# A decoder layer on one core: two weight splits moved into the merge and kept in DRAM, an engine order written out at the end of the mix

## The chip, the core and the metric

The kernel runs on one core of a Trainium2 chip. The core has five engines with a queue of instructions each: PE (TensorE, matrix products), DVE (VectorE, element by element), ACT (ScalarE, functions and scalings), POOL (GpSimd, element by element) and SP (SyncE, which here only starts DMA transfers). ACT and POOL can start DMA transfers too. Each engine runs its own queue in order and waits for the others through semaphores. SBUF is the on-chip memory of 128 partitions; PSUM holds the products in banks of 128 x 512 float32. DRAM is reached by DMA only. The metric is the device time of one execution in microseconds (us); less is better.

## The reference

One layer of a decoder on x of 1024 positions by 1024 channels, all in float32:

```python
xn = rmsnorm(x, norm_mix_w[l])
proj = xn @ w_in[l]
da_q, da_k, da_v, sw_q, sw_k, sw_v, g_da, g_sw = split_cols(proj)
...
y_da = diff_attention(da_q, da_k, da_v, lam, lam_init, subln_w[l])
y_sw = sliding_window_attention(sw_q, sw_k, sw_v, sinks[l])
merged = jax.nn.sigmoid(g_da) * (y_da @ w_br_da[l]) + jax.nn.sigmoid(g_sw) * (y_sw @ w_br_sw[l])
x = x + merged @ w_mix_out[l]
xn = rmsnorm(x, norm_ffn_w[l])
x = x + conv_ffn(xn, w_up[l], conv_w[l], conv_b[l], w_down[l])
return rmsnorm(x, norm_final_w)
```

`conv_ffn` is `u = xn @ w_up` (1024 to 5632), a causal convolution of width 3 along the positions, `silu(gate) * val`, and `@ w_down`. The change lies in the lines of `merged`, of `merged @ w_mix_out` and at the start of `xn @ w_up`.

## The kernel before, in words

**Products.** Channels lie on the partitions, positions along the free axis, in two halves (`hf` 0 and 1) of 512. A float32 product is made of three products of a faster type: each operand is split into a high part (a cast, on ACT) and a low part (what the cast left out, a subtraction, on DVE), and hi x hi, hi x lo and lo x hi are added in PSUM. `split`, `load_w` (L177 and L179) and `part_pair` (L125 and L127) make such parts; they are called splits below. On top of it stands one level of Strassen-Winograd: a product of 2 x 2 blocks takes seven block products P1 to P7 instead of eight, of operands that are blocks (A11, A12, A22; B11, B21, B22) or sums of blocks (S1 to S4; T1 to T4).

**Stages.** By time in the trace: projection (0 to 235), attention (to 507), merge (to 594.7), mix (to 672.5), the pairs of the up product (to 1107), the down product (to 1331). 

**Merge** (`rest`). Eight steps m, one per 128 channels. SP loads two stored gates `gr` (L845), POOL multiplies them by the rstd (L846), ACT takes the sigmoid, PE makes the two branch products (`sc`, `g`), DVE multiplies the gates into them as it takes them out of PSUM (L860, L862), POOL (DVE for the last two) adds the two branches to `mr` (L870), and ACT and DVE split what the mix needs (L883, L884). `add_on` (L890) adds blocks of `mr` with a DMA that adds into its destination ("accumulating"), started by POOL.

**Mix** (`mix`). Seven stages in the order P1, P2, P5, P6, P3, P7, P4, each in two half stages i of two output blocks m; i runs from 0 to 13. A block is 12 matmuls of 512 columns. Two sets of four PSUM banks (`chains`) take the stages by turns so that some of them accumulate onto the one before; P4 follows P7 in the same four banks, each of which has to be taken out by DVE first (an *eviction*, L1040: x plus or minus the bank, into `xm`). After the last eviction of a block half, `finish` stores it to DRAM (`x2d`, L935, started by ACT), squares it (ACT, L942) and adds the square to `rstd` (POOL, L943). From the finished blocks the operands of the up product are made: `scale1` to `scale4` scale them (ACT, L952, L958, L965), `sum2`, `sum3` and others add them (L931), and `put` splits them (L919, or L922 and L923 with a factor). The table `due` says at which half stage each of these is written; `tc.issue_after` and `tc.high_priority` bind the scheduler, which otherwise orders each engine's queue by itself.

**Pairs** (`hidden`). The up product has 22 pairs j (a block of `gate` and one of `val`), seven products of 12 matmuls each. For j=0 the weights are split in four parts by `part_pair` at the end of the mix; j=0 also takes the column sums of the squares (`col_sums`, L206: 16 matmuls of one column), from which the rstd comes that the output is scaled by. For j=0 and 1 the sums S1 to S4 of the weights have been made in DRAM during attention, by 8 copies (SP, L108) and 8 accumulating DMAs (POOL, L109) in `sums_up`.

**Order around the change.** Each engine works through its queue in order, so an eviction on DVE waits for everything written ahead of it there. PE's P4 block m waits for the eviction of P7's block m; j=0's first four products take the banks of P4's four blocks and wait for their evictions.

## Time and profile before

| | us |
|---|---|
| three runs | 1333.22, 1335.96, 1336.31 |
| median | 1335.96 |
| the profiled execution | 1333.29, of which the span is 1331.1 |
| PE busy | 1303.5 of the span |
| merge, 507 to 595 | PE busy 88.0 of 88 |
| end of mix and j=0, 660 to 707 | PE waits at four places, 8.5 in all |
| pairs, 707 to 1107 | PE busy 400 of 400 |

How to read it: a row of a timeline has its start in us from the start of the span, its length, the engine, the line of the kernel, the operation, out<-in by the program's names, the shapes, how many instructions in a row it stands for, and in brackets the idle time before it and who ended that. Matmuls of one row overlap, so their lengths add up to more than the time between starts. Windows give busy time of each engine in a stretch, with the number of instructions in brackets, then the clock granted to PE as a share of the full one, the share of the DMA engines that was busy, and GB/s.

### The profile page before, as it was taken

Reading aid. Unit: us, or ns where it says so; the run is one execution under the profiler, and the core shown is the slowest. Engines: PE = TensorE matmul, PEld = TensorE weight load, DVE = VectorE, ACT = ScalarE, POOL = GpSimd, SP = SyncE. Lnnn points to the kernel's source line nnn. Section 1 sums busy time; section 2 is a strip of 40 time slices with the busy share of each in tenths; the row PEclk is TensorE's granted clock in tenths of the full one; section 3 lists DMA queues with packets and bytes.
Section 4 is the critical chain, followed back from the end, with each engine's and each line's share of the span. In section 5 each row is a group of like instructions: output and inputs, shape, how many; then the busy total and the mean of one; then the engine's idle time right before and its main releaser. Section 6 shows DMA issues by size and latency. Waiting matters only on the chain.

```text
span 1331.1 us, 17305 instructions
## 1 busy us (share of the span) xinstructions
PE 1303.5 (98%) x6162; PEld 1083.9 (81%) x6162; DVE 1086.7 (82%) x1510; ACT 638.0 (48%) x1010; POOL 518.4 (39%) x405
## 2 busy tenths in 40 slices
PE   9999999999999999999979999999999999999997
PEld 7888888887898778888858888888888888888886
DVE  8846675288888977666898999999999999896865
ACT  9432232266667765335664433434343335554543
POOL 0448663001111015743374667676667632000002
PEclk9999999999999999999989999999999999999999
DMA  7346665978674336569352434663636237953534
GB/s 291 126 178 166 227 213 149 270 181 235 153 162 123 116 119 205 166 181 292 128 178 103 182 136 121 171 209 102 188 123 164 78 103 254 331 182 117 166 97 146
DMA packets 84293, 227.47 MB, mean 171 GB/s; under 512 B 9328, under 2 KB 17136, under 8 KB 83952
## 3 DMA queue, kind: packets, MB, share of 16 engines
q1 hardware_dynamic: 63264, 187.04, 41.4%
q0 software_dynamic: 8064, 22.02, 9.8%
q10 hardware_dynamic: 12880, 17.31, 3.7%
q8 instruction: 48, 0.79, 0.2%
q14 instruction: 37, 0.30, 0.1%
HBM read 173.39 MB, written 84.41 MB: 194 GB/s over the span
## 4 chain that ended last, share of the span: by engine, by line
PE 74%; DVE 13%; issue 6%; DMA 3%; ACT 2%; POOL 1%; SPq 0%; POOLq 0%; ACTq 0%; DVEq 0%
PE t L1064 25%; PE y L1284 9%; PE d L1284 7%; PE m L1037 5%; PE g L198 4%; PE g L199 4%; PE g L200 4%; PE sc L688 3%; DVE wl L158 2%; DVE c L1230 2%; DVE c L1231 1%; PE t L704 1%; PE sc L198 1%; PE sc L200 1%; PE sc L199 1%
## 5 line engine op out<-in xcount | busy, mean ns | idle before, releaser
L179 DVE TENSOR_TENSOR wl<-raw,wh 128x1024 fp32r<-128x1024 f32 (+2 forms) x91 | 109.5, 1204 | 44.3 <-ACT wh L177 34.7
L177 ACT CAST wh<-raw 128x1024 fp32r<-128x1024 f32 (+2 forms) x91 | 80.6, 886 | 107.2 <-PE y L1284 44.2
L1214 POOL TENSOR_TENSOR us<-us,rstd 128x1024 f32<-128x1024 f32 x42 | 94.1, 2316 | 48.9 <-DVE us L519 32.5
L1064 PE MATMUL t<-T,sh 128*128 128x512 f32 x352 | 110.4, 395 | 0.0
L215 POOL TENSOR_TENSOR rs<-ms,mhalf 128x8 f32<-128x8 f32 (+2 forms) x9 | 14.3, 1588 | 237.7 <-DVE ms L213 232.8
L1228 ACT ACTIVATE c<-us,vecs 128x1024 f32<-128x1024 f32 x44 | 54.7, 1247 | 101.8 <-POOL us L1214 96.7
L142 POOL TENSOR_TENSOR sf<-rv 128x512 f32<-128x512 f32 x29 | 61.1, 2108 | 100.3 <-DMA rv<-in_w_up 48.1
L156 ACT CAST sh<-sf 128x1024 fp32r<-128x1024 f32 x58 | 60.5, 1044 | 74.3 <-PE t L1064 41.0
L158 DVE TENSOR_TENSOR sl<-sf,sh 128x1024 fp32r<-128x1024 f32 x58 | 81.7, 1408 | 11.5 <-ACT sh L156 11.5
L1064 PE MATMUL t<-x,wh 128*128 128x512 f32 x248 | 82.8, 390 | 0.7 <-DVE x L923 0.7
L1064 PEld LDWEIGHTS t<-T,sh 128*128 128x128 f32 x352 | 67.1, 191 | 14.0
L198 PE MATMUL g<-xh,wh 128*128 128x512 f32 x176 | 70.9, 403 | 2.7 <-ACT g L617 2.7
L1231 DVE SCALAR_TENSOR_TENSOR c<-us,vecs,c 128x1024 f32<-128x1024 f32 x44 | 72.2, 1674 | 0.1
L199 PE MATMUL g<-x,wh 128*128 128x512 f32 x176 | 70.5, 400 | 0.0
L200 PE MATMUL g<-xh,wl 128*128 128x512 f32 x176 | 70.4, 400 | 0.0
L158 DVE TENSOR_TENSOR wl<-raw,wh 128x1024 fp32r<-128x1024 f32 x29 | 70.0, 2412 | 0.1
L1064 PE MATMUL t<-T,sl 128*128 128x512 f32 x176 | 69.5, 395 | 0.0
L1064 PE MATMUL t<-x,sh 128*128 128x512 f32 x212 | 68.2, 389 | 0.0
L1230 DVE SCALAR_TENSOR_TENSOR c<-us,vecs,c 128x1024 f32<-128x1024 f32 x44 | 66.1, 1535 | 1.5 <-ACT c L1228 1.4
L144 POOL TENSOR_TENSOR sf<-raw,rv 128x512 f32<-128x512 f32 x29 | 51.8, 1786 | 35.5 <-DVE sl L158 35.5
L671 POOL MEMSET aT<- 128x128 f32 x32 | 7.3, 247 | 149.4 <-PE t L717 39.4
L1284 PE MATMUL y<-h,wh 128*128 128x512 f32 (+1 forms) x224 | 65.3, 375 | 0.0
(342 smaller groups left out, 4010.3 us busy)
## 6 DMA issues: line engine op xcount, KB each, us to landing
u<-qd SPq DMA_DIRECT2D x72, 256.0 KB, 6.0
raw<-in_w_in SPq DMA_DIRECT2D x22, 512.0 KB, 5.6
raw<-in_w_up SPq DMA_DIRECT2D x22, 512.0 KB, 5.0
hd<-c SPq DMA_DIRECT2D x22, 512.0 KB, 2.6
sdP<-in_w_down POOLq DMA_DIRECT2D x16, 704.0 KB, 9.4
rv<-in_w_up SPq DMA_DIRECT2D x20, 512.0 KB, 3.6
hc<-hd SPq DMA_DIRECT2D x33, 256.0 KB, 5.7
gr<-gd SPq DMA_DIRECT2D x16, 512.0 KB, 4.4
```

What stands on the lines that cost most here:

```text
L158: low = nc.vector.tensor_tensor(lo, src, hi.bitcast(F32), ALU.subtract)
L177: self.hi = nc.scalar.copy(wh, raw)
L179: self.lo = (eng or nc.vector).tensor_tensor(wl, raw, wh.bitcast(F32), ALU.subtract)
L198: nc.tensor.matmul(ps, wh[:, kc + o, :], ah, start=first and n == 0, stop=False)
L199: nc.tensor.matmul(ps, wh[:, kc + o, :], al, start=False, stop=False)
L200: nc.tensor.matmul(ps, wl[:, kc + o, :], ah, start=False, stop=last and n == len(kcs) - 1)
L1037: nc.tensor.matmul(ps, v[:, m % 2 * 4 + k, :], x, start=start and k == j == 0, stop=k == 3 and j == 2, skip_group_check=True)
L1064: nc.tensor.matmul(ps, (ah, ah, al)[p][:, k, :], (bh, bl, bh)[p], start=first and n == p == 0, stop=last and p == 2 and n == len(ks) - 1, ...
L1214: i = (nc.vector if m % NF == 0 else nc.gpsimd).tensor_tensor(us[:, 2:], us[:, 2:], self.rstd, ALU.mult)
L1230: nc.vector.scalar_tensor_tensor(c, us[:, 1:T + 1], cw[1], c, ALU.mult, ALU.add)
L1231: nc.vector.scalar_tensor_tensor(c, us[:, 0:T], cw[0], c, ALU.mult, ALU.add)
L1284: nc.tensor.matmul(ps, v[:, k - k0, :], x, start=start and k == i == 0, stop=k == HK - 1 and i == 2, skip_group_check=True)
```

## The change

It does five things.

1. `sums_up` is gone from attention, with its 16 DMAs.
2. A generator `ahead_parts` runs in the merge's steps m = 0 to 5, two calls a step. It loads the weights of P4 and of pairs 0 and 1 (six loads of 512 KB, SP), splits P4's weights and pair 0's blocks and sums (six casts on ACT, six subtractions and eight sums on DVE), and stores the parts to DRAM (six stores of high parts by ACT, six of low parts by SP), and pair 1's raw sums (two stores, SP). The cast goes into a buffer `yh` of which there is one.
3. P4's weights and pair 0's are then loaded as parts (`load_halves`, `pre_pair`: four and seven loads of 512 KB), with no cast and no subtraction at the end of the mix.
4. From the end of the mix on, every operation of `mix` on DVE and ACT is bound to the one before it on its engine (`chain`), in the order of a new table `due`, keyed by half stage and block. All of `sum3` is on DVE (before: half of it on POOL), `sum2` and four of the additions of squares are accumulating DMAs (before: POOL). Pair 0's products come in the order P1, P5, P3, P7, P6, P2, then the column sums, then P4 (before: P1, P5, P3, P7, P2, column sums, P6, P4).
5. The two sets of PSUM banks change places.

```diff
+            elif nk == "halves":
+                self.wq.append(self.load_halves(src, "raw" if src is self.md4[0] else None))
...
-    def sums_up(self):
...
+    def load_halves(self, src, tag=None, pool=None, tags=("wh", "wl"), shape=[P, KC, P]):
+
+        r = []
+        for d, t in zip(src, tags):
+            x = self.tl(self.wp, shape, tag, F32R, bufs=RAW) if tag else self.tl(pool or self.wp, shape, t, F32R)
...
+    def ahead_parts(self, pool):
...
+        def cut(t, hi, lo, n=T):
+            h = self.tl(pool, [P, T], "yh", F32R, bufs=1)
+            x, r = t[:, T - n:], h[:, :n]
+            nc.scalar.copy(r, x)
+            nc.scalar.dma_start(hi, r.bitcast(F32))
+            tt(x.bitcast(F32R), x, r.bitcast(F32), ALU.subtract)
+            late.append(lambda: nc.sync.dma_start(lo, x))
...
+        def steps():
+            w = [load(self.w_mix[4 + 2 * h:6 + 2 * h, :, 4:8, :].rearrange("m p k c -> p m k c")) for h in range(2)]
+            yield
+            for h in range(2):
+                cut(w[h], *self.md4[h])
                 yield
+            g, v = load(self.w_up[0]), load(self.w_up[NF])
+            yield
+            a, b = sums(g, v)
+            yield
+            for t, d in ((g, self.ud0[0]), (a, self.ud0[1]), (b, self.ud0[2])):
+                cut(t, *d)
+                yield
+            cut(v, self.ud0[3][0, :, :H2], self.ud0[3][0, :, H2:], H2)
+            g, v = load(self.w_up[1]), load(self.w_up[1 + NF])
+            yield
+            a, b = sums(g, v)
...
                 for m in range(KC):
...
+                    if m:
+                        next(ahead, None)
                     ps = self.tl(self.psS, [P, T], "sc")
...
+                    next(ahead, None)
...
+                if m > 3 and hf == 0:
+                    nc.gpsimd.dma_start(a, sq, accum_op=ALU.add)
+                else:
+                    nc.gpsimd.tensor_tensor(a, a, sq, ALU.add)
...
-        sum3 = lambda k: add(col(k, 1), c22(k), nc.vector if k < 2 else nc.gpsimd)
-        sum2 = lambda k: add(col(k, 0), c22(k))
...
+        sum3 = lambda k: add(col(k, 1), c22(k))
+        sum2 = lambda k: nc.gpsimd.dma_start(col(k, 0), c22(k), accum_op=ALU.add)
...
+        due = {(5, 1): ((scale1, 0, 1),), (6, 1): ((scale1, 2, 3),), (9, 1): ((scale2, 0, 1), (t1, 0, 1)), (10, 0): ((scale4, 0), (sum2, 0)),
...
-            chains = [[self.tl(psM, [P, H2], "m") for _ in range(4)] for _ in range(2)]
+            chains = [[self.tl(psM, [P, H2], "m") for _ in range(4)] for _ in range(2)][::-1]
...
+    def chain(self, tails, n, f, *a):
+
+        with self.tc.issue_after(tails[n]):
+            i = f(*a)
+        tails[n] = i.ins
+        return i
...
-                    for n, i in enumerate((0, 2, 4, 3, 1)):
+                    for i in (0, 2, 4, 3, 5, 1):
```

Every chained operation stands on one line of the changed kernel, L1126, whatever it does; the tile tells them apart.

**DVE from P7's first evictions on.** In these rows `xm` with `m` is an eviction, B_k and T_k are splits of B22 and T1, `x` is a split of T3, `xm` with `c` is `sum3`, `xm` alone is `scale2`'s add. The piece before lies between the split of P4's second weights and P4's first eviction:

```order
L920 TENSOR_TENSOR B_0_5756<-c_5775,B_0_5756 128x512
L920 TENSOR_TENSOR B_1_5757<-c_5775,B_1_5757 128x512
L1040 TENSOR_TENSOR xm_5769<-xm_5769,m_5788 128x512
L1040 TENSOR_TENSOR xm_5770<-xm_5770,m_5789 128x512
L920 TENSOR_TENSOR T_2_5754<-xm_5765,T_2_5754 128x512
L920 TENSOR_TENSOR T_3_5755<-xm_5766,T_3_5755 128x512
L920 TENSOR_TENSOR x_1091_6338<-xm_5763,x_1091_6338 128x512
L920 TENSOR_TENSOR x_1092_6341<-xm_5764,x_1092_6341 128x512
L920 TENSOR_TENSOR B_2_5758<-c_5776,B_2_5758 128x512
L920 TENSOR_TENSOR B_3_5759<-c_5776,B_3_5759 128x512
L1040 TENSOR_TENSOR xm_5767<-xm_5767,m_5786 128x512
```

Changed, from P7's first eviction up to the split ahead of its last:

```order
L1126 TENSOR_TENSOR xm_5812<-xm_5812,m_5827 128x512
L1126 TENSOR_TENSOR B_0_5801<-c_5820,B_0_5801 128x512
L1126 TENSOR_TENSOR xm_5813<-xm_5813,m_5828 128x512
L1126 TENSOR_TENSOR xm_5810<-xm_5810 128x512
L1126 TENSOR_TENSOR xm_5811<-xm_5811 128x512
L1126 TENSOR_TENSOR T_2_5799<-xm_5810,T_2_5799 128x512
L1126 TENSOR_TENSOR T_3_5800<-xm_5811,T_3_5800 128x512
L1126 TENSOR_TENSOR xm_5814<-xm_5814,m_5829 128x512
L1126 TENSOR_TENSOR B_1_5802<-c_5820,B_1_5802 128x512
L1126 TENSOR_TENSOR xm_5808<-xm_5808,c_5820 128x512
L1126 TENSOR_TENSOR xm_5809<-xm_5809,c_5820 128x512
L1126 TENSOR_TENSOR x_1103_6357<-xm_5808,x_1103_6357 128x512
```

Before, the third and the fourth block were evicted one behind the other; now at least one split stands between two evictions, and the split B_k is of the block that was evicted just before it.

**ACT in the same place.** For two of P7's blocks before: two scalings, two casts, then casts of pair 0's weights and P4's first store:

```order
L958 ACTIVATE c_5776<-xm_5769,vecs 128x512
L958 ACTIVATE c_5776<-xm_5770,vecs 128x512
L919 CAST B_2_5758<-c_5776 128x512
L919 CAST B_3_5759<-c_5776 128x512
L125 CAST sh_6356<-raw_6354 128x1024
L125 CAST wh_6394<-raw_6392 128x1024
L935 DMA x2d<-xm_5767 128x512
```

Changed, for P7's first two blocks (xm_5812 and xm_5813):

```order
L1126 DMA x2d<-xm_5812 128x512
L1126 ACTIVATE sqs<-xm_5812 128x512
L1126 ACTIVATE c_5820<-xm_5812,vecs 128x512
L1126 CAST B_0_5801<-c_5820 128x512
L1126 DMA x2d<-xm_5813 128x512
L1126 ACTIVATE sqs<-xm_5813 128x512
L1126 ACTIVATE xm_5810<-xm_5810,ms_5822 128x512
L1126 ACTIVATE xm_5811<-xm_5811,ms_5822 128x512
L1126 CAST T_2_5799<-xm_5810 128x512
L1126 CAST T_3_5800<-xm_5811 128x512
```

The store and the square of each evicted block now stand ahead of its scaling and cast, and no cast of weights is left there.

**POOL at the end of the mix.** Before, from the squares of P4's first two blocks on:

```order
L943 TENSOR_TENSOR rstd<-rstd,rv_6327 128x512 x2
L931 TENSOR_TENSOR xm_5763<-xm_5763,xm_5767 128x512
L931 TENSOR_TENSOR xm_5764<-xm_5764,xm_5768 128x512
L943 TENSOR_TENSOR rstd<-rstd,rv_6326 128x512 x2
L931 TENSOR_TENSOR xm_5765<-xm_5765,xm_5769 128x512
L931 TENSOR_TENSOR xm_5766<-xm_5766,xm_5770 128x512
```

Changed, from the square of P7's last block on:

```order
L1018 TENSOR_TENSOR rstd<-rstd,sqs 128x512
L1041 DMA xm_5810<-c_5821 128x512
L1016 DMA rstd<-rv_6381 128x512
L1041 DMA xm_5811<-c_5821 128x512
L1016 DMA rstd<-rv_6381 128x512
L1038 TENSOR_TENSOR xm_5808<-xm_5808,xm_5812 128x512
L1016 DMA rstd<-rv_6380 128x512
L1038 TENSOR_TENSOR xm_5809<-xm_5809,xm_5813 128x512
L1016 DMA rstd<-rv_6380 128x512
L1038 TENSOR_TENSOR xm_5810<-xm_5810,xm_5814 128x512
```

The four DMA rows into `rstd` add the squares of P4's blocks into one tile; the column sums read that tile.

**DVE in the merge.** A step before (the split of the step's weights, one of `mr`, four gates):

```order
L179 TENSOR_TENSOR wl_5289<-raw_5285,wh_5287 128x1024
L884 TENSOR_TENSOR x_968_5282<-mr,x_968_5282 128x512
L862 TENSOR_TENSOR gr_5291<-gr_5291,sc_5299 128x512
L860 SCALAR_TENSOR_TENSOR gr_5291<-gr_5291,sc_5299 128x512
L862 TENSOR_TENSOR gr_5295<-gr_5295,g_5326 128x512
L860 SCALAR_TENSOR_TENSOR gr_5295<-gr_5295,g_5340 128x512
```

Changed, a step and a half:

```order
L931 TENSOR_TENSOR gr_5293<-gr_5293,sc_5306 128x512
L929 SCALAR_TENSOR_TENSOR gr_5293<-gr_5293,sc_5306 128x512
L140 TENSOR_TENSOR yr_5302<-yr_5302,yh_5385 128x1024
L931 TENSOR_TENSOR gr_5297<-gr_5297,g_5333 128x512
L140 TENSOR_TENSOR yr_5365<-yr_5365,yh_5449 128x1024
L929 SCALAR_TENSOR_TENSOR gr_5297<-gr_5297,g_5347 128x512
L242 TENSOR_TENSOR wl_5375<-raw_5371,wh_5373 128x1024
L955 TENSOR_TENSOR x_983_5362<-mr,x_983_5362 128x512
L140 TENSOR_TENSOR yr_5366<-yr_5366,yh_5468 128x1024
L931 TENSOR_TENSOR gr_5377<-gr_5377,sc_5389 128x512
L929 SCALAR_TENSOR_TENSOR gr_5377<-gr_5377,sc_5389 128x512
```

L140 is the subtraction of `cut`. It stands between the gates (L929, L931); a gate behind it waits until ACT has made its cast into `yh`.

More of the change, by code (lines that the diff above doesn't have):

```diff
@@ L503, in project, with recombine @@
         self.uw = None
-    def recombine(self, ps, us, tp, o, after=None, pre=False):
+    def recombine(self, ps, us, tp, o, after=None):
         nc = self.nc
@@ L565, in attention @@
             nc.sync.dma_start(self.bias, self.bias_d)
-            later, sums = [], self.sums_up()
+            later = []
             st = self.q_stacks(0), self.kv_stacks(0)
@@ L588, in attention @@
                             self.da_av(u, i // 2, aT, y)
-                            with tc.issue_after(self.sync), tc.issue_after(self.sum):
-                                next(sums, None)
                     else:
@@ L839, in rest @@
                 mr = mp.tile([P, KC, T], F32, name="mr")
+                ahead = self.ahead_parts(yrp)
                 for m in range(KC):
@@ L876, in rest @@
                         self.add_on(mr, m - 4, 0, m - 4, 1)
+                    next(ahead, None)
+                assert next(ahead, 0) == 0
             self.pctx.close()
@@ L998, in mix @@
                 for h in range(2):
[L999 to L1005 removed]
+                    with tc.high_priority(60), tc.issue_after(tails[0]) if i > 8 else nullcontext(), tc.issue_after(tails[1]) if i > 8 else nullcontext():
+                        w = self.next_w(3 if i > 9 else 2)
+                    if i < 11:
+                        tails[:] = self.lo.ins, self.hi.ins
                     if n == 0:
@@ L1008, in mix @@
                             nc.sync.dma_start(xm[m], self.xT[m])
-                    run_due(i)
-                    held = lows[-1] if lows else None
-                    first = self.lo
-                    if i == 12:
-                        self.uw = uw
-                        w0.update(self.part_pair(pair, 1))
-                        self.uw = None
+                    for f, *ks in due.pop((i - 1, 1), ()):
+                        for k in ks:
+                            f(k)
                     if h == 0:
```

150 lines of the change are left out of this document (87 added, 63 removed).

## The prediction

> **What bounds the kernel now.** I read the page first, then a table of windows by stage, then the timelines of the engines where TensorE (PE) stops.
>
> ```profile
> span 1331.1 us, 17305 instructions
> ...
> PE 1303.5 (98%) x6162; PEld 1083.9 (81%) x6162; DVE 1086.7 (82%) x1510; ACT 638.0 (48%) x1010; POOL 518.4 (39%) x405
> ```
>
> PE is busy 98% of the span, so a gain must come from the 27.6 us in which it idles or from a low clock. The windows say where (merge, the end of the layer's first half, the pairs):
>
> ```profile
> core 0: us, PE busy (x) PEld busy (x) DVE busy (x) ACT busy (x) POOL busy (x), PEclk, DMA share, GB/s
> 507.00:595.00 88.00, 88.00 (x390) 72.88 (x389) 56.65 (x55) 33.32 (x38) 56.84 (x27) 1.00 0.60 178
> ...
> 673.00:707.00 34.00, 27.27 (x102) 21.55 (x103) 29.89 (x30) 17.59 (x28) 21.88 (x15) 0.80 0.52 178
> 707.00:1107.00 400.00, 400.00 (x1771) 331.38 (x1769) 389.54 (x337) 159.79 (x174) 253.92 (x178) 1.00 0.44 137
> ```
>
> The merge, into which work is moved, has a PE without a gap; the pairs have none either. The loss lies at the end of the mixing product and in pair j=0. PE there, in order of time:
>
> ```profile
> 659.95 0.61 PE L1037 MATMUL m<-x,wh 128*128 128x512 f32 x2
> ...
> 666.80 0.70 PE L1037 MATMUL m<-x,wh 128*128 128x512 f32 x2 [1.25 <-DVE xm L1040]
> ...
> 675.97 0.70 PE L1064 MATMUL t<-B,wh 128*128 128x512 f32 x2 [3.47 <-DVE xm L1040]
> 679.70 0.79 PE L1064 MATMUL t<-B,wl 128*128 128x512 f32 x1 [3.03 <-DVE wl L127]
> ...
> 686.77 0.61 PE L1064 MATMUL t<-B,sh 128*128 128x512 f32 x2
> ...
> 689.49 0.61 PE L1064 MATMUL t<-x,sh 128*128 128x512 f32 x2
> ...
> 695.65 0.50 PE L1064 MATMUL t<-x,wh 128*128 128x512 f32 x1 [0.73 <-DVE x L923]
> ...
> 696.22 2.24 PE L206 MATMUL t<-ones,rstd 128*128 128x1 f32 x16
> 698.32 1.20 PE L1064 MATMUL t<-T,sh 128*128 128x512 f32 x2
> ...
> 706.71 0.62 PE L1064 MATMUL t<-B,wh 128*128 128x512 f32 x2
> ```
>
> Stage P4 starts at 659.95. One block of 12 matmuls takes 2.72 us (686.77 to 689.49), so P4's four end at 670.8 and j=0's seven with the column sums take 21.3 more: j=1 could start at 692.1 and starts at 706.71. This 14.6 us is the most that the change can win: 8.5 in the four waits, the rest in low clock:
>
> ```profile
> 678.00:684.00 6.00, 4.30 (x10) 3.40 (x11) 6.00 (x6) 5.55 (x10) 4.95 (x3) 0.51 0.70 193
> ...
> 698.00:704.00 6.00, 6.00 (x16) 4.76 (x16) 2.40 (x4) 1.74 (x2) 0.19 (x2) 0.50 0.41 152
> ```
>
> What PE waits for is VectorE (DVE), which has a backlog:
>
> ```profile
> 649.27 0.69 DVE L1040 TENSOR_TENSOR xm<-xm,m 128x512 f32<-128x512 f32 x1 [2.03 <-PE m L1037]
> ...
> 664.78 1.28 DVE L920 TENSOR_TENSOR B<-c,B 128x512 fp32r<-128x512 f32 x2
> 665.98 1.27 DVE L1040 TENSOR_TENSOR xm<-xm,m 128x512 f32<-128x512 f32 x2
> ...
> 668.38 3.49 DVE L920 TENSOR_TENSOR x<-xm,x 128x512 fp32r<-128x512 f32 x2
> ...
> 675.15 0.68 DVE L1040 TENSOR_TENSOR xm<-xm,m 128x512 f32<-128x512 f32 x1
> 675.75 1.69 DVE L127 TENSOR_TENSOR sl<-raw,sh 128x1024 fp32r<-128x1024 f32 x1
> ...
> 679.57 2.30 DVE L127 TENSOR_TENSOR sl<-raw,sh 128x1024 fp32r<-128x1024 f32 x1
> ...
> 687.00 0.67 DVE L1040 TENSOR_TENSOR xm<-xm,m 128x512 f32<-128x512 f32 x1
> ```
>
> The same 512-wide subtraction takes 0.64 us at 664.78 and 1.74 at 668.38. In the second case GpSimd (POOL) runs a two-operand add beside it:
>
> ```profile
> 653.86 1.29 POOL L943 TENSOR_TENSOR rstd<-rstd,sqs 128x512 f32<-128x512 f32 x1 [0.71 <-ACT sqs L942]
> ...
> 667.84 3.49 POOL L943 TENSOR_TENSOR rstd<-rstd,sqs 128x512 f32<-128x512 f32 x2 [5.27 <-ACT sqs L942]
> ```
>
> Both slow down when they meet. An eviction from PSUM keeps its 0.68.
>
> **The change, part by part: the end of the mix.** Taken from DVE between 655 and 698: two splits of P4's weights (1.2 each) and four of j=0 (1.69, 1.69, 2.30, 0.68). Taken from POOL: four sums and four additions of squares, now accumulating DMAs. That removes most of the collisions. The loads in place of the splits (4 and 7 of 512 KB, 5.8 MB) mostly run after P7, and there the DMA engines are nearly free:
>
> ```profile
> 660.00:676.00 16.00, 11.29 (x50) 8.76 (x48) 16.00 (x16) 9.67 (x15) 10.66 (x7) 1.00 0.18 66
> ```
>
> I cost them at nothing; if they were late, P1's weights would be the first missed. The order of the banks costs nothing: both versions give each j=0 product a bank of the same stage.
>
> What replaces the backlog is the fixed order. Each eviction of P7 and P4 on DVE now stands behind operations that need ScalarE's (ACT) work on the *previous* eviction. ACT's rows:
>
> ```profile
> 654.49 1.05 ACT L177 CAST wh<-raw 128x1024 fp32r<-128x1024 f32 x1 [0.77 <-PE m L1037]
> ...
> 668.19 1.32 ACT L958 ACTIVATE c<-xm,vecs 128x512 f32<-128x512 f32 x2
> 669.42 1.13 ACT L919 CAST B<-c 128x512 fp32r<-128x512 f32 x2
> ...
> 676.23 0.63 ACT L942 ACTIVATE rv<-xm 128x512 f32<-128x512 f32 x1 [3.79 <-DVE xm L1040]
> ```
>
> An eviction ends at 675.83 and its Square starts at 676.23 (0.40, the store's issue between); the next ACT operation starts 0.54 later; a scaling is 0.66, a cast 0.57, a DVE subtraction 0.60 to 0.64. From the end of one eviction to the end of the next:
> - P7 m0 to m1: 0.40 + 0.54 + 0.66 + 0.57 + 0.64 + 0.68 = 3.5.
> - m1 to m2: 0.40 + 0.54 + 0.66, an add 0.64, a cast 0.57, two subtractions 1.24, 0.68 = 4.7.
> - m2 to m3: 2.17 as above to B22's cast, then subtraction, add, the cast that follows that add, its subtraction, eviction: 5.3.
> - m3 to P4 m0: 2.17, three DVE operations 1.86, 0.68 = 4.7. P4 m0 to m1: four operations, 5.3.
> - m1 to m2: 0.94, two casts, a scaling, 0.64, 0.68 = 4.0. m2 to m3: 4.2.
>
> None is as short as PE's 2.72. The start: P3's last eviction ends 649.96; 0.94 and a cast of 1.05 on ACT, the split 1.21, two adds, two subtractions and the eviction (1.24 + 1.28 + 0.68) put P7 m0's end at 656.4. The others follow at 659.9, 664.6, 669.9, 674.6, 679.9, 683.9 and 688.1. The last stood at 687.67 before. So PE waits about 1.9 us ahead of P4 m3, then 2.0, 2.6, 1.3, 1.5 ahead of j=0's first four products: 9.3 us where it was 8.5. P7, P6 and P2 end at 696.4, which is where the column sums started before.
>
> The column sums now wait for four accumulating DMAs into one tile, each behind the last. The nearest row is the merge's and the mix's accumulation of 256 KB:
>
> ```profile
> DMA to landing us min/median/max: 3.3/6.7/8.7
> ```
>
> The first can start with P4 m0's square, 674.6 + 0.9. At 3.3 each nothing waits; at 6.7 they end at 702.3, 6 us late. In the mix most took near 5.5, which I take: 697.5. With 2.24 for the sums and the one product left (2.72, or 5.3 as after 698.32), j=1 starts between 701.3 and 710; with 5.5 and the low clock at 705.0. Two more terms: meetings with the POOL adds that are left, 1 us (two at half of the 1.1 seen), and low clock between 670 and 690, 0 to 4 us since PE would be slower just where it waits anyway; I take 0.5. That is 706.5, so **-0.2 us**, with ends -5.4 and +8.
>
> The row on the clock: after a gap of only 0.73 us and the sparse column sums the clock fell to 0.50. The Trainium skill ("TensorE: Matmul & The Clock Gate", "Why this matters for your kernels") says that the clock stays up where no gap between bursts exceeds about 3 us. By that rule no wait of mine would lower it. The trace agrees in the first low stretch, which follows gaps of 3.47 and 3.03 us, and not in the second. A clock that stays up would take 3.1 us (2.6 and 0.5) off the sum, 1335.2 in the end; I give that 3 in 10, inside the forecast's case.
>
> **The merge.** It gains about 10 MB of DMA (6 loads and 14 stores), 5.9 us of ACT, and on DVE five 1024-wide subtractions, one 512-wide and eight 512-wide sums over five of its eight steps of 10.88 us. Its rows:
>
> ```profile
> 536.43 4.75 POOL L846 TENSOR_TENSOR gr<-gr,rstd 128x1024 f32<-128x1024 f32 x2 [0.69 <-DMA gr<-gd]
> 541.24 2.39 POOL L870 TENSOR_TENSOR mr<-gr,gr 128x1024 f32<-128x1024 f32 x1
> ```
> ```profile
> 543.66 0.80 SPq L845 DMA_DIRECT2D gr<-gd  x2
> ```
> ```profile
> 541.38 3.34 DVE L179 TENSOR_TENSOR wl<-raw,wh 128x1024 fp32r<-128x1024 f32 x1 [0.22 <-ACT wh L177]
> ...
> 545.91 0.69 DVE L862 TENSOR_TENSOR gr<-gr,sc 128x512 f32<-128x512 f32 x1 [0.59 <-PE sc L200]
> ...
> 587.99 1.21 DVE L179 TENSOR_TENSOR wl<-raw,wh 128x1024 fp32r<-128x1024 f32 x1
> ```
>
> A 1024-wide subtraction takes 1.21 alone and 3.34 while POOL's 7.14 us per step hold it up. DVE has 56.65/88, or 7.0 us of work in a step. Added at the low price: 5 x 1.21 + 9 x 0.64 = 11.8, 2.4 a step: 9.4 of 10.88, no cost. At the high one (3.34, and 1.74 for 512): 32.4, 6.5 a step: 13.5, five times 2.6 late, 13 us, less about 6: the gate at 545.91 uses what POOL had multiplied by 538.8 (the first of the pair at 536.43), with one sigmoid of about 1 us between. POOL meets DVE in 7.14/10.88 = 66% of the time; so weighted, 2.6 and 1.4, it is 25.6, 5.1 a step, 12.1 of 10.88, and 6 us late: as much as the slack. POOL's own loop (its next gates load when its add ends, 543.66) has no slack of its own, and doubled traffic and split stores ahead of those loads on SP's queue lengthen it too. I take **+2.5 us**, nearer to the covered end, with ends 0 and +9.
>
> Attention loses 16 DMAs from SP and POOL, which were behind a full PE: nothing.
>
> **Sum.** 1333.29 of the profiled execution (span 1331.1 and 2.2 around it) - 0.2 + 2.5 = 1335.6. That execution is 2.7 below the median of the three, 1335.96; the forecast for the median is 1338.3.
>
> **The rivals.**
> - *The backlog was all* (faster). If the accumulations take 4 us or less, the clock stays up and the merge has its cover, j=1 starts at 701.3 to 703 and the time is 1329 to 1332. It speaks for it that DVE loses 8.8 us of splits, against it that my chain has no DVE backlog in it at all and is still as long. It decides at an eviction interval under 4 us.
> - *The merge falls behind*: the high price, or a cast that waits until its single buffer's store has left. PE waits 8 us or more by the fourth step: 1344 to 1348. For it: 10 MB in five steps ask DMA for 184 GB/s on top of the stage's 178. Against it: the sigmoid's slack.
> - *The serial accumulations decide*: at 6.7 us or above, with low clock before, the column sums start after 702: 1342 to 1347.
> - *The change doesn't act*: only if the new order left DVE's backlog as it was. The splits are gone from it, so I give that no chance.
>
> **How the numbers follow.** Forecast case (1334 to 1343): 0.45. Faster rival: 0.23. Merge: 0.20. Accumulations: 0.12. A measurement here can tell about 0.3%, 4 us: faster is under 1332, slower over 1340. The first case gives 0.28 same and 0.17 slower, the faster rival 0.21 faster and 0.02 same, the others 0.32 slower: 0.21, 0.30, 0.49. The range, 1329 to 1348, reaches into both sides.
>
> **What would show it.** Right: DVE idle 1.5 to 2.5 us ahead of each B22 subtraction, released by ACT; PE waits of 1 to 3 us each for evictions at the six places; the column sums released by a DMA into rstd; short PE waits in the merge. Wrong: DVE still full between 660 and 690, or evictions less than 4 us apart, or a merge with a gap over 8 us.

## The result, and the profile after

The changed kernel takes 1344.93 us (median of four runs, 1343.95 to 1346.08), the kernel before 1335.28 beside it (four runs). The ratio is 1.0075, with a 95% interval of 1.0057 to 1.0092: 9.65 us slower. Each of the two executions that were profiled lies up to 2 us from its median, so that their spans differ by 11.1.

The two profiled executions, cut at PE's first matmul of each stage (us), with their difference:

| from, to | before | after | difference |
|---|---|---|---|
| start, merge | 507.63 | 502.50 | -5.1 |
| merge, mix | 87.04 | 102.97 | +15.9 |
| mix, pair 1 | 112.04 | 110.87 | -1.2 |
| pair 1, end of span | 624.39 | 625.86 | +1.5 |
| span | 1331.1 | 1342.2 | +11.1 |

The page of the changed kernel has PE still at 98%, and DVE and POOL with less work than before (1086.7 and 518.4 there):

```profile
PE 1310.3 (98%) x6162; PEld 1088.1 (81%) x6162; DVE 1076.0 (80%) x1520; ACT 638.8 (48%) x1010; POOL 496.8 (37%) x395
```

So the time isn't lost to an engine with more work over the whole span. PE's rows of the changed kernel show where it stands (brackets: the idle time before a matmul, and who ended it), first in the merge:

```profile
535.13 0.79 PE L261 MATMUL g<-yh,wh 128*128 128x512 f32 x1 [5.27 <-DVE gr L931]
551.43 0.50 PE L261 MATMUL g<-yh,wh 128*128 128x512 f32 x1 [0.38 <-DVE gr L929]
564.71 0.80 PE L261 MATMUL g<-yh,wh 128*128 128x512 f32 x1 [4.83 <-DVE gr L931]
```

then at the end of the layer's first half:

```profile
682.48 0.96 PE L1099 MATMUL m<-x,wh 128*128 128x512 f32 x2 [2.64 <-DVE xm L1126]
...
692.78 0.95 PE L1138 MATMUL t<-T,sh 128*128 128x512 f32 x2 [2.44 <-issue]
...
701.88 0.73 PE L1138 MATMUL t<-x,sh 128*128 128x512 f32 x2 [1.80 <-DVE xm L1126]
...
711.81 1.84 PE L269 MATMUL t<-ones,rstd 128*128 128x1 f32 x16
```

The merge had no wait before and now has 10.5 us of them, for gates. After the two long ones PE runs at a low clock. The windows of the changed kernel (the clock is the third number from the right):

```profile
core 0: us, PE busy (x) PEld busy (x) DVE busy (x) ACT busy (x) POOL busy (x), PEclk, DMA share, GB/s
...
535.00:541.00 6.00, 5.87 (x17) 4.68 (x18) 3.33 (x6) 1.18 (x2) 3.22 (x1) 0.63 0.93 275
...
565.00:571.00 6.00, 6.00 (x16) 4.69 (x16) 5.46 (x6) 1.07 (x2) 2.98 (x2) 0.57 0.83 280
```

5.87 us at 0.63 and 6.00 at 0.57 lose 2.2 and 2.6 us against a full clock; with the waits that is 15.3 of the merge's 15.9.

DVE's rows ahead of the two waits:

```profile
529.83 4.64 DVE L140 TENSOR_TENSOR yr<-yr,yh 128x1024 fp32r<-128x1024 f32 x1 [2.46 <-ACT yh L138]
534.40 0.67 DVE L931 TENSOR_TENSOR gr<-gr,g 128x512 f32<-128x512 f32 x1
...
562.63 1.43 DVE L140 TENSOR_TENSOR yr<-yr,yh 128x512 fp32r<-128x512 f32 x1 [3.80 <-ACT yh L138]
563.98 0.68 DVE L931 TENSOR_TENSOR gr<-gr,g 128x512 f32<-128x512 f32 x1
```

Both times a gate that PE waits for stands behind a subtraction of `cut`. The first subtraction starts 2.46 us late, after ACT's cast, and then takes 4.64, with POOL's multiplication of two gates beside it, as a row of POOL shows:

```profile
528.40 4.98 POOL L913 TENSOR_TENSOR gr<-gr,rstd 128x1024 f32<-128x1024 f32 x2
```

(It waits for POOL rather than running slower; the last section shows this.) The second waits 3.80 for a cast, and ACT's rows say why:

```profile
556.41 0.33 ACTq L139 DMA_DIRECT2D ud<-yh  x1
561.98 0.62 ACT L138 CAST yh<-yr 128x512 fp32r<-128x512 f32 x1 [5.60 <-DMA ud<-yh]
```

The cast waits 5.60 for the store of the part before it to leave the one buffer `yh`. That is the second reason that the prediction gave for a late merge.

A third thing differs from the start of the merge on. The loads of the first step's gates, and POOL's multiplication of them, in the kernel before and in the changed one:

```profile
488.55 4.88 SPq L845 DMA_DIRECT2D gr<-gd  x2
492.17 2.40 POOL L846 TENSOR_TENSOR gr<-gr,rstd 128x1024 f32<-128x1024 f32 x1 [7.36 <-DMA gr<-gd]
```
```profile
502.14 0.86 SPq L912 DMA_DIRECT2D gr<-gd  x2
511.04 4.78 POOL L913 TENSOR_TENSOR gr<-gr,rstd 128x1024 f32<-128x1024 f32 x2 [30.49 <-DMA gr<-gd]
```

Before, POOL began 15.5 us ahead of the merge's first matmul; now it begins 8.5 us behind it. In every kernel below that has splits in the merge it begins 6 to 11 us behind. So the lead that POOL had over PE is gone; what that alone costs, no run shows.

At the end of the layer's first half, DVE does what the prediction's sums had:

```profile
666.84 0.68 DVE L1126 TENSOR_TENSOR xm<-xm,m 128x512 f32<-128x512 f32 x1
669.85 0.69 DVE L1126 TENSOR_TENSOR B<-c,B 128x512 fp32r<-128x512 f32 x1 [2.34 <-ACT B L1126]
670.46 0.68 DVE L1126 TENSOR_TENSOR xm<-xm,m 128x512 f32<-128x512 f32 x1
672.85 1.94 DVE L1126 TENSOR_TENSOR xm<-xm 128x512 f32<-128x512 f32 x2 [1.70 <-ACT xm L1126]
...
679.10 0.69 DVE L1126 TENSOR_TENSOR B<-c,B 128x512 fp32r<-128x512 f32 x1 [2.34 <-ACT B L1126]
```

It idles 2.3 us ahead of each of the four splits of B22, released by ACT. Behind the last three of them PE stands until the next eviction is done.

Attention had eight PE waits, 7.95 us together, and has seven with 2.56 now. The largest piece of the 5.1 us that it wins is one wait. In the kernel before, PE waited there for ACT, and ACT for a weight load:

```profile
313.19 0.39 PE L716 MATMUL t<-aT,v 128*128 128x256 f32 x1 [2.97 <-ACT aT L706]
```
```profile
310.80 1.04 ACT L177 CAST wh<-raw 128x1024 fp32r<-128x1024 f32 x1 [3.50 <-DMA raw<-in_w_in]
```
```profile
302.40 1.78 SPq L108 DMA_DIRECT2D ud<-ud  x2
304.28 0.53 SPq L167 DMA_DIRECT2D raw<-in_w_in  x1
```

The load stood on SP's queue behind two of the copies of `sums_up`. The change removed the copies, and this wait is gone.

### The profile page after: what moved, and what is told of

Same layout as the page of the kernel before. It is cut to its first block, busy times and chain, and to the rows that moved or that the text cites. A ratio compares the mean times of both kernels' runs of the same rounds, so it can differ in the third digit from the quotient of the medians.

```text
span 1342.2 us, 17333 instructions
## 1 busy us (share of the span) xinstructions
PE 1310.3 (98%) x6162; PEld 1088.1 (81%) x6162; DVE 1076.0 (80%) x1520; ACT 638.8 (48%) x1010; POOL 496.8 (37%) x395
## 4 chain that ended last, share of the span: by engine, by line
PE 77%; DVE 9%; issue 5%; DMA 3%; ACT 3%; POOL 2%; ACTq 0%; SPq 0%; POOLq 0%; DVEq 0%
PE t L1138 32%; PE y L1359 9%; PE d L1359 7%; PE m L1099 4%; PE g L261 3%; PE g L262 3%; PE g L263 3%; PE sc L754 3%; DVE c L1305 2%; DVE wl L221 1%; PE t L770 1%; DMA gr<-gd 1%; PE sc L842 1%; PE t L873 1%; DVE c L1306 1%
## 5 line engine op out<-in xcount | busy, mean ns | idle before, releaser
L242 DVE TENSOR_TENSOR wl<-raw,wh 128x1024 fp32r<-128x1024 f32 (+2 forms) x89 | 96.5, 1085 | 55.8 <-ACT wh L240 46.2
L1138 PE MATMUL t<-T,sh 128*128 128x512 f32 x364 | 113.1, 394 | 2.4 <-issue 2.4
L205 POOL TENSOR_TENSOR sf<-rv 128x512 f32<-128x512 f32 x29 | 58.4, 2014 | 101.8 <-DMA rv<-in_w_up 44.3
```

The source lines that it names most:

```text
L242: self.lo = (eng or nc.vector).tensor_tensor(wl, raw, wh.bitcast(F32), ALU.subtract)
L1138: nc.tensor.matmul(ps, (ah, ah, al)[p][:, k, :], (bh, bl, bh)[p], start=first and n == p == 0, stop=last and p == 2 and n == len(ks) - 1, ...
```

## The experiments

Each kernel ran beside the kernel before; the ratio is against it. Stage lengths (us, from the first matmul of each stage, as above) come from one profiled execution of each kernel, which lies up to 2.7 us from that kernel's median:

| kernel | ratio, 95% interval | merge | mix to pair 1 | pair 1 to end |
|---|---|---|---|---|
| before | 1 | 87.0 | 112.0 | 624.4 |
| after | 1.0075 [1.0057, 1.0092] | 103.0 | 110.9 | 625.9 |
| E1 no work in the merge | 0.9961 [0.9946, 0.9976] | 88.7 | 112.3 | 626.3 |
| E2 second cast buffer | 1.0042 [1.0026, 1.0059] | 97.8 | 112.3 | 631.1 |
| E3 gates first | 1.0092 [1.0072, 1.0112] | 107.0 | 109.1 | 627.4 |
| E4 before, no sums in attention | 0.9937 [0.9922, 0.9952] | 87.0 | 110.4 | 625.8 |
| E5 subtractions after evictions | 1.0071 [1.0056, 1.0086] | 100.5 | 113.0 | 627.0 |
| E6 the same, flushed in time | 1.0054 [1.0039, 1.0069] | 103.9 | 111.0 | 625.3 |
| E7 only P4's parts in the merge | 1.0013 [1.0001, 1.0026] | 93.1 | 112.6 | 628.9 |
| E8 new order, old weights | 1.0006 [0.9993, 1.0019] | 87.0 | 112.6 | 629.0 |
| E9 = E6 and squares on POOL | 0.9989 [0.9971, 1.0007] | 101.4 | 99.2 | 630.1 |
| E10 = E9, second buffer, old banks | 0.9969 [0.9953, 0.9985] | 97.8 | 101.9 | 628.1 |
| E11 = E1, old banks | 0.9955 [0.9938, 0.9971] | 87.0 | 110.6 | 628.6 |
| E12 = E10, spread over the steps | 0.9978 [0.9961, 0.9995] | 98.1 | 102.1 | 628.8 |

**E1: the merge without its new work.** It leaves out the loads, splits and stores of `ahead_parts`; what is loaded later has the same size and other values.

```diff
-                ahead = self.ahead_parts(yrp)
+                for a in range(2):
+                    nc.sync.dma_start(self.any[a], parts[0][a].bitcast(F32))
...
-                    next(ahead, None)
```

> The changed kernel without the work in the merge: nothing is loaded, split, summed or stored there but two stores of 512 KB; P4's weights and pair 0's are loaded from those (other values), pair 1's sums are read from the up weights themselves. If all of the loss lies in the merge's work: the merge goes from 103.2 back to 87 us, the attention keeps its 5.2 us gain, the end keeps its 45.6, the whole is near 1329. If the end or the attention had depended on it: they move by more than 2 us.

Measured 1330.05 us, 0.9961: the merge is back at 88.7, 1.7 us above the kernel before, and pair 1 to the end still has its 1.9 us more. The new work in the merge is the loss, and the rest of the change by itself wins 5 us.

**E2: a second buffer for the cast.** `cut` alternates between `yh` and two half tiles.

```diff
-            h = self.tl(pool, [P, T], "yh", F32R, bufs=1)
+            if len(turn) % 2:
+                pieces = [(0, self.tl(pool, [P, T], "yh", F32R, bufs=1)[:, :n])]
+            else:
+                pieces = [(c, self.tl(self.gpool, [P, H2], "g", F32R, bufs=2)) for c in range(0, n, H2)]
...
```

> The changed kernel with a second buffer for the casts of the merge (every other cast goes, in two halves of 512, into a tile that attention has left free). If the single buffer holds up the casts, and behind them gates and PE: the second stall of 4.83 us (gate behind a cast that waits 5.6 us for the store) and the low clock after it go, 5 to 7 us less, 1338 to 1340. If POOL's loop decides (its step is 13.9 to 17.4 us instead of 10.87): less than 2 us.

The 4.83 us wait is gone, and 5.1 of the merge's 15.9 with it. The first wait stays at 4.06, and waits of 2.50 and 1.97 stand at 551 and 568. So the single buffer is a third of the loss. The kernel's ratio falls by 0.0033, about 4.4 us, a little less than expected.

**E3: the gates ahead of the new work.** Each portion of `ahead_parts` is bound behind the step's last gate.

```diff
-                    if m:
-                        next(ahead, None)
...
-                    next(ahead, None)
+                    with tc.issue_after(last.ins):
+                        for _ in range(2 if m else 1):
+                            next(ahead, None)
```

> The changed kernel with the same work in the merge, but each step's two portions are written behind the step's four gates instead of around its products. Order theory (a subtraction that waits stands ahead of a gate on DVE, and PE waits for the gate's bank): the stalls of 5.3 and 4.8 us and the low clock behind them go, 12 to 16 us less, 1329 to 1333. Volume theory (port, DMA and engine time of the added work are too much wherever it stands): within 4 us of the changed kernel's 1344.9.

The theory that DVE's order alone makes the loss fell: the merge became 4 us longer. The long waits for gates went (one of 1.45 is left), and others came. In SP's queue of this kernel the load of a gate now stands behind stores of low parts, and POOL waits for it:

```profile
532.95 3.19 SPq L141 DMA_DIRECT2D md<-yr  x2
536.24 1.49 SPq L912 DMA_DIRECT2D gr<-gd  x1
```
```profile
544.18 2.37 POOL L913 TENSOR_TENSOR gr<-gr,rstd 128x1024 f32<-128x1024 f32 x1 [5.79 <-DMA gr<-gd]
```

With POOL late, ACT's cast of `mr` is late, and on DVE the split of `mr` stands ahead of that of the step's own weights:

```profile
549.53 0.69 DVE L955 TENSOR_TENSOR x<-mr,x 128x512 fp32r<-128x512 f32 x1 [6.18 <-ACT x L954]
```

So the splits of the weights come late, and PE waits 6.56 and 7.28 for them. Moved off the gates on DVE, the new work stands ahead of the step's own on SP's queue.

**E4: the kernel before without the sums in attention.** Left out are the 16 DMAs of `sums_up`; pairs 0 and 1 read raw rows in place of the sums.

```diff
-            later, sums = [], self.sums_up()
+            later = []
...
-                            with tc.issue_after(self.sync), tc.issue_after(self.sum):
-                                next(sums, None)
```

> The kernel before without the 16 DMAs in attention that make the sums of pairs 0 and 1 (these pairs read the up weights themselves instead, other values). If those DMAs cost the attention its 5.2 us: 1330, the wait of 2.97 us at 313 gone. If the attention was shortened by another ordering of the scheduler: within 1.5 us of before.

1327.66 us, 7.5 less. The merge starts at 503.22 instead of 507.63, as in the changed kernel. The 16 DMAs weren't hidden: attention's gain is theirs. (4.4 of the 7.5 us lie in attention; the rest lies behind the merge, in one profiled execution, and was not looked into.)

**E5 and E6: DVE's subtractions behind the evictions.** The low parts of the B, T and x operands are held back until the next eviction has been issued. E6 limits this to the half stages 10 to 13:

```diff
+        def low(f, *a):
+            if 9 < i < 14:
+                held.append((f, *a))
+            else:
+                vec(f, *a)
...
-                vec(tt, lo, src, hi.bitcast(F32), ALU.subtract)
+                low(tt, lo, src, hi.bitcast(F32), ALU.subtract)
...
                         vec(tt, x, x, ps, ALU.subtract if o or stage == "P2" else ALU.add)
+                        flush()
```

> The changed kernel with one thing moved: from P7 on, DVE's subtraction of a split stands behind the next eviction instead of ahead of it; ACT's order is as it was. Round-trip theory: evictions come at about 3 us instead of 4.7, PE's waits of 0.5 to 2.6 us before j=0 shrink, P4's start to j=1 goes from 45.6 to 38 to 41 us, 5 to 7 us less in all. Rival, that ACT itself is full there (about 20 us of work in 22): less than 2 us.

> As e6_defer, but no subtraction is held back behind the last eviction, so that T2's last split doesn't come after all of T4's (PE waited 11.6 us for it there). Round-trip theory: from mix start to j=1 101 to 105 us instead of 110.9, 1335 to 1339. Rival, that ACT is full: above 1342.

In E5 a split that a later addition waits for was held too long (one low part of T2 is there made from a block already changed), and PE waited 11.58 us for a T; it tells little. In E6 the evictions of P4 start at 680.90, 683.87, 686.27 and 688.74, 2.4 to 3.0 apart where they had been 4.1 to 5.4, and mix to pair 0's first product falls from 81.8 to 76.6 us. Yet pair 1 starts no earlier. The gain went into one new wait, in PE's row, and the low clock behind it. The wait is for the accumulations on POOL:

```profile
708.85 3.57 PE L269 MATMUL t<-ones,rstd 128*128 128x1 f32 x16 [8.18 <-DMA rstd<-rv]
```
```profile
683.02 0.86 POOL L1029 DMA_DIRECT2D rstd<-rv  x1 [1.76 <-ACT rv L1140]
...
693.13 0.89 POOL L1029 DMA_DIRECT2D rstd<-rv  x1 [5.95 <-issue]
...
705.61 0.87 POOL L1029 DMA_DIRECT2D rstd<-rv  x1 [2.88 <-issue]
```

The four (three are shown) are issued 5 to 10 us apart, the later ones each after a wait of POOL's queue. In the changed kernel the same series ended before PE got there.

**E7: P4's parts alone.** Pairs 0 and 1 are left out of `ahead_parts`, and their loads read other values. (`steps` ends behind the two cuts of `w_mix`.)

> The changed kernel with only P4's two portions cut in the merge; pair 0 is loaded from two stored tiles of other values, pair 1 reads raw weights, and their loads, sums, casts and stores are left out. If the loss goes with the amount of added work: about a third of the 16 us stays, 1333 to 1336. If single places decide: the stall of 5.3 us in step 1 (second cut of P4) with its low clock stays whole, the one of 4.8 goes, 1336 to 1339.

The merge takes 93.1: 6 us stay with P4's two loads and cuts, and 10 go with the pairs' part. That is a little more than the third that the first expectation had. The stall of 5.3 in the second expectation isn't there: waits for gates of 1.02, 0.78 and 0.17 stand in its place, then 1.44 for a split and 0.74 for a gate. The time, 1338.72, lies in the second's range, but only 1.1 us above what the kernel before took beside it (1337.63), so it can't decide between the two.

**E8: the new order with the old weights.** Splits and sums as before (the sums' DMAs in the sliding-window part of attention), with the changed kernel's fixed order and E6's deferral.

> The order alone: the new order at the end of the mix, with subtractions behind the next eviction, on the weights as before (P4's and pair 0's split at the end of the mix, nothing added in the merge). The 16 DMAs for pairs 0 and 1 stay in attention but are started in its later, sliding-window part. Theory that the ping-pong was the price of the order and the DMAs' place the price in attention: merge 87, mix start to j=1 104 to 108, attention 3 to 5 us shorter, 1321 to 1327. Rival, that without the move of the splits the DVE backlog is back: 110 or more, 1328 to 1333.

No change, 1.0006. PE's rows of this kernel name ACT's weight casts in place of evictions:

```profile
668.33 1.20 PE L1047 MATMUL m<-x,wh 128*128 128x512 f32 x4 [3.05 <-ACT wh L177]
...
694.61 1.95 PE L206 MATMUL t<-ones,rstd 128*128 128x1 f32 x16 [2.04 <-DMA rstd<-rv]
...
706.63 1.22 PE L1089 MATMUL t<-B,wh 128*128 128x512 f32 x2 [5.63 <-ACT wh L125]
```

The first cast stands on ACT behind the store and the square of one of P7's blocks; the second waits 7.29 us itself, for a load of pair 1's sums. The column sums wait for a DMA into `rstd`, the sign that the prediction gave. So this order with the splits in place wins nothing, but the accumulating DMAs are in it too, and the same kernel with all squares added by POOL (as in E9) was not run. Nor did the sums' DMAs win anything in their new place: the wait of 2.97 us in attention is gone, waits of 0.98 and 1.50 stand elsewhere, and the merge starts at 506.97, 0.7 us sooner.

**E9: E6, with all squares added by POOL.**

```diff
-                if m > 3 and hf == 0:
-                    nc.gpsimd.dma_start(a, sq, accum_op=ALU.add)
-                else:
-                    nc.gpsimd.tensor_tensor(a, a, sq, ALU.add)
+                nc.gpsimd.tensor_tensor(a, a, sq, ALU.add)
```

> The new kernel with two edits at the layer's end: the DVE subtractions of the low parts of T2 and T3 wait until the next eviction has been issued, and all squares are summed by POOL additions, none by an accumulating DMA. Theory 'DVE's order, then the accumulations': with the subtractions out of the way the products of mix up to pair 0's first group took 76.6 us instead of 81.8, and the 5 us reappeared as 8.2 us of waiting for a DMA into rstd; with no DMA in the sum that wait is gone, mix to pair 1's first matmul falls from 110.9 to 101 to 104 us, and the kernel is 6 to 9 us faster than the new one (ratio 1.001 to 1.004 against the kernel before). The merge stays at 101 to 104 us. Rival 'POOL is full there': POOL's additions of 256 KB halves cost what the DMAs did, the wait returns with POOL or DVE named in place of the DMA, and the stretch stays within 2 us of 110.9.

Mix to pair 1 falls to 99.2 us, 11.7 under the changed kernel. PE has one wait left there, and none ahead of the column sums:

```profile
688.28 0.50 PE L1149 MATMUL t<-B,sl 128*128 128x512 f32 x1 [1.85 <-DMA sl<-ud]
...
698.87 1.84 PE L269 MATMUL t<-ones,rstd 128*128 128x1 f32 x16
```

In DVE's rows the eviction now comes first, and the idle 2.3 us are gone:

```profile
678.35 0.68 DVE L1137 TENSOR_TENSOR xm<-xm,m 128x512 f32<-128x512 f32 x1
678.95 0.68 DVE L1137 TENSOR_TENSOR B<-c,B 128x512 fp32r<-128x512 f32 x1
679.55 0.68 DVE L1137 TENSOR_TENSOR x<-xm,x 128x512 fp32r<-128x512 f32 x1
680.71 1.29 DVE L1137 TENSOR_TENSOR xm<-xm,c 128x512 f32<-128x512 f32 x1 [0.48 <-ACT c L1137]
```

So the subtraction ahead of the eviction, then the accumulations, bounded this stretch, in this order. But the kernel, at 0.9989, can't be told from the kernel before: the merge is still 14.4 us longer than there, and 4.2 us come back after pair 1's start, at the turn from the pairs to the down product:

```profile
1111.96 1.19 PE L1370 MATMUL y<-sh,wh 128*128 128x512 f32 x2 [3.03 <-DVE us L587]
```
```profile
1111.00:1116.00 5.00, 4.04 (x10) 3.20 (x11) 5.00 (x7) 1.24 (x2) 0.00 (x0) 0.51 1.02 383
```

The wait was 0.53 before and 1.74 in the changed kernel; the low clock behind it was in neither. It takes 3.0 us (5.96 us of PE at half the clock, in a window of the last section).

**E10: E9 with the second cast buffer and the banks in the old order; E12: the same with the portions spread over all eight steps** (`if m in (2, 4, 6)` in place of `if m` ahead of the products).

> The edits of the run before, a second cast buffer in the merge, and the two groups of banks of the last mixing product in the order that they had in the kernel before. Each of three causes gives back its own: the second cast buffer 5 us of the merge (97.8 in its own run), the end of the layer 7 to 9 us, and the banks about 1 to 3 us at the start of mix. Theory 'they add up': 12 to 17 us under the new kernel, so 3 to 8 us under the kernel before (ratio 0.994 to 0.998). Rival 'the end's gain needs the merge's lateness': no faster than the kernel before.

> As the second run of this set, with the portions of the splitting spread over all eight steps of the merge instead of two in each step from the second pair on. Theory 'the portions stand too close': the merge falls below the 97.8 us that a second cast buffer alone gave, to 90 to 95, and the kernel is 3 to 8 us faster than the second run. Rival 'the same engine work in the same window': the merge stays at 96 to 99 us, since DVE, ACT and POOL have the same sum of work there.

E10 takes 1333.12 us against 1336.88: 0.9969, 0.3% under the kernel before and about 1% under the changed one. It is the fastest of the kernels that compute the whole layer. Merge 97.8 as with the buffer alone, mix to pair 1 101.9 (2.7 more than E9, with 2.5 us of new waits at mix's start), and 628.1 after. E12's merge is as long as E10's (98.1), so the portions' spacing isn't what holds the merge. About 10.7 us of it are left unexplained by any run. In E10's rows they show in POOL's loop: from the third step to the eighth its pairs of multiplications (L919) start at 526.77 and 594.10, 67.3 us apart, where the kernel before had 525.64 and 582.24, 56.6. Whether the late start of that loop, its loads on SP or its meetings with DVE stretch it was not tested.

**E11: E1 with the banks in the old order.**

```diff
-            chains = [[self.tl(psM, [P, H2], "m") for _ in range(4)] for _ in range(2)][::-1]
+            chains = [[self.tl(psM, [P, H2], "m") for _ in range(4)] for _ in range(2)]
```

> The kernel without the work in the merge (it leaves out the splitting of the last mixing product's and the up projection's weights there, and reads other values in their place), with the banks in the order of the kernel before. With banks swapped and no work in the merge, mix to pair 0's first product took 85.1 us, and PE stood at mix's start for a group that the merge's last gates still read. Theory 'the swap has a price that the late merge hid': that stretch falls to 81.5 to 83.5 us and the ratio from 0.996 to 0.993 to 0.995. Prediction on record (the bank order costs nothing): 85 us stays, ratio 0.996 within 0.001.

Mix to pair 0's first product falls from 85.1 to 83.4, as the first expectation had it, with a wait of 1.25 at mix's start where there were 1.01 and 1.63, and the merge is 1.7 shorter. But the time (0.9955 against 0.9961) is that of the second: of 3.4 us that are won up to pair 1, 2.3 come back after it. In E10, with the old order too, waits of 0.68 and 1.68 stand at the same place; in the changed kernel, with the new order and a late merge, none does. The bank order stays open, within about 3 us.

## Why the prediction was right or wrong, step by step

The side was right (slower had the largest chance) and the time lies in the range, but 6.6 us above the forecast, and by the case that had 2 in 10, the merge that falls behind.

- *Merge, +2.5 with ends 0 and +9*: **mis-sized; it measured +15.9.** The step that failed is the one that priced the new work as load against slack (12.1 of 10.88 us a step, less 6 us of the sigmoid's slack). The slack wasn't there: POOL's first multiplication came 8.5 us behind the merge's start, where it had come 15.5 us ahead of it, and DVE waited 4.86 us for the sigmoid of the first gate (514.57). The loss shows as single waits: a gate behind one subtraction, for which DVE stood idle 2.46 us and which then took 4.64. The high price, 3.34, was a subtraction's wait for one instruction of POOL; here POOL had two in a row. The cast that waits for its store was named in the rival, with a condition and no price; E2 gives it 5 us. The rival's sign, 8 us of waits by the fourth step, came in the fifth (5.7, then 10.5). And two gaps of about 5 us each brought a low clock worth 4.8 us that the sum didn't have. What makes the other 10 us is open: E3 and E12 moved the same work and didn't shorten the merge, E7 took most of it out and did.
- *POOL's loop, no slack*: right as to the mechanism. E3 shows a load of its gates delayed by stores on SP, and in E10 the loop is as much longer as the merge.
- *Attention, nothing*: **wrong; -5.1**, and E4 shows -4.4 of merge start without any other edit. "Behind a full PE" didn't hold: PE had 7.95 us of waits in this stage, 2.97 of them in one place, and the cover was never looked for on SP's queue, where the copies stood ahead of a weight load.
- *End of mix and pair 0, -0.2*: -1.2, right as to the chain, and by luck as close as that. PE's waits came to 7.6 us, at five places with 0.2 to 2.6, where the sum had 9.3, and the column sums weren't late; against that, the low clock took 5.1 us (three stretches of 3.4 us at half the clock) where the sum had 3.1. Evictions came 3.6, 5.6, 5.7, 4.8, 5.4, 4.1 and 5.0 us apart, for 3.5, 4.7, 5.3, 4.7, 5.3, 4.0 and 4.2; the second is longer since POOL ran beside it (1.94 for two additions). E6 confirms that ACT's chain through the subtraction sets these intervals: without it they are 2.4 to 3.0.
- *Accumulations, 5.5 each and about 1 us late*: each was shorter, as the answer for their line in the changed kernel says, and the column sums didn't wait:

```profile
DMA to landing us min/median/max: 3.2/3.8/5.3
```

  The sign that a DMA would release them didn't show; the late evictions hid it, and in E6 (8.18 us) and E8 (2.04) it shows.
- *Loads in place of splits, nothing*: held, with one wait of 1.85 in E9.
- *Bank order, nothing*: not settled (E11).
- *Clock*: the prediction gave the rule of the Trainium skill ("TensorE: Matmul & The Clock Gate", "Why this matters for your kernels"), no loss while gaps stay under about 3 us, 3 chances in 10. The changed kernel's windows speak against it in this place: after the gap of 2.64 us the clock was 0.57, after 2.44 again 0.57, after 1.80 it was 0.67. The last section shows what the gaps have in common.

```profile
682.50:686.50 4.00, 4.00 (x11) 3.15 (x12) 1.75 (x3) 2.38 (x4) 2.10 (x2) 0.57 1.03 296
692.80:696.80 4.00, 4.00 (x11) 3.14 (x12) 2.55 (x4) 2.89 (x5) 1.62 (x2) 0.57 0.90 197
701.90:705.90 4.00, 4.00 (x12) 3.19 (x13) 2.13 (x3) 3.67 (x7) 2.08 (x2) 0.67 0.56 137
```

The remaining +1.5 us, after pair 1's start, is mostly the wait at the turn to the down product (1.74 for 0.53). What sets it is not settled.

## What to carry to other kernels

Work moved into a stage with a full PE has to be priced by its place in each queue: what stands behind it on DVE, ACT and SP, and which buffer it waits for, before its sum is set against slack. A fixed order is worth what its longest cross-engine chain allows; put the eviction that PE waits for ahead of whatever needs another engine's answer. And DMAs on a queue that also issues loads are not free because the compute engine is busy: look for the load behind them. Leaving them out helped (E4), and moving them within the stage did not (E8).

## What the runs showed of the hardware

- Gaps of the same length had different ends. The wait of 3.03 us at the turn to the down product was followed by half the clock in E9, and by the full clock in E10:

```profile
1110.42 0.70 PE L1376 MATMUL y<-sh,wh 128*128 128x512 f32 x2 [3.03 <-ACT x L960]
```

  What tells them apart is where the gap lies. In each trace the clock changes only at multiples of 3.41 us from its first change, and between full and half. In the changed kernel the low stretches are 532.62 to 539.45, 563.35 to 570.17, 682.81 to 686.23, 693.05 to 696.47 and 703.29 to 706.71, each one or two such steps long. Windows cut at these steps, first E9, then E10:

```profile
1107.68:1111.09 3.41, 1.25 (x6) 0.71 (x4) 3.41 (x5) 1.96 (x2) 0.92 (x1) 1.00 0.93 291
1111.09:1117.92 6.83, 5.96 (x14) 4.74 (x15) 5.12 (x7) 1.24 (x2) 0.00 (x0) 0.50 1.00 369
```
```profile
1105.46:1108.88 3.42, 1.93 (x9) 1.27 (x7) 3.38 (x6) 1.79 (x2) 1.60 (x1) 1.00 0.99 296
1108.88:1112.29 3.41, 1.87 (x8) 1.60 (x9) 3.41 (x5) 1.42 (x3) 0.00 (x0) 1.00 1.04 380
```

  E9's gap lies within one step, in which PE is busy for 37% of the time; E10's is shared by two steps with 56% and 55%. The fourteen traces bear this out: from 60 us on, and without the steps that hold one-column matmuls (as the column sums), 42 steps stand ahead of a fall, in none of which PE is busy for more than 47% of the time, and 4919 aren't followed by one, none of them under 48%. (A step with the column sums fell in the kernel before at 79%, 694.09; there the one-column matmuls are counted as busy.) This is read from the traces, and no run was made to test it.
- A 1024-wide subtraction on DVE that took 1.21 us alone took 4.64 in the changed kernel and 6.84 in E3 while POOL ran two-operand work of the same width. It waits, it doesn't run slower: POOL's two multiplications from 528.40 on end at 533.38, and the subtraction at 534.47. Of DVE's two-operand instructions (`TENSOR_TENSOR`) between 495 and 720 us in the fourteen traces, 272 took longer than alone, and each ended 0.55 or 0.56 us (512 wide) or 1.08 or 1.09 us (1024 wide) after an instruction of POOL had ended. None of them reads PSUM. So the price is what is left of POOL's instruction, or of several in a row.
- An accumulating DMA of 256 KB into `rstd` landed after 3.2 to 5.3 us in the changed kernel, and in E6 after:

```profile
DMA to landing us min/median/max: 3.2/5.6/9.5
```
